# Four gate projections of each mixer as column pairs of seven half products, in a two-layer hybrid decoder trunk

## The chip, the core and the metric

The kernel runs on one core of a Trainium2 chip. The metric is the device time of one execution in microseconds (us), lower is better; of several runs the median counts. Engines are named as the profile names them: PE is TensorE (matrix products), PEld its weight loads, DVE VectorE, ACT ScalarE, POOL GpSimd, SP SyncE (which issues the weight transfers here).

## What is computed

A decoder trunk of two layers on 512 tokens, with 16 learned meta tokens ahead of them, 528 in all, and 1024 channels. A layer is a mixer and a gated MLP, each with an RMS norm before and behind it. The mixer projects its input once; the columns of that projection belong to four retention heads (with rotary positions on query and key) and four heads of gated linear attention (GLA). Every head's output is normalised and multiplied by a swish gate, `silu(rg)` or `silu(gr)`, which are columns of the same projection.

```python
proj = h @ w_in                       # 1024 -> 3600 columns
rq, rk, rv, rg, gq, gk, gv, gr, ga = jnp.split(proj, offs, axis=-1)
rq, rk = _rope(rq, pos), _rope(rk, pos)
o_ret = _head_group_norm(_retention(rq, rk, rv), ret_norm_w) * jax.nn.silu(rg)
log_a = jax.nn.log_sigmoid(ga @ gla_gate_w2 + gla_gate_b) / GLA_TAU
o_gla = _head_rms_norm(_gla(gq, gk, gv, log_a), gla_norm_w) * jax.nn.silu(gr)
m = jnp.concatenate([o_ret, o_gla], axis=-1) @ w_out
h = h + _rmsnorm(m, post_mix_norm)
u = causal_conv3(_rmsnorm(h, pre_ffn_norm) @ ffn_up)
a, g = jnp.split(u, 2, axis=-1)
h = h + _rmsnorm((gelu(a) * g) @ ffn_down, post_ffn_norm)
```

## The kernel before

**Precision and tiles.** Channels lie on the partitions, tokens in the free dimension. Each float32 operand of a large product is held as a high and a low float16 part, and a product of two such operands is three matmuls for each block of 128 input channels (`product_step`, L523 to L525). A tile of the mixer's projection is 128 columns of `w_in`, one head's `rk`, `rq`, `rv`, `rg` and so on. It is made in two halves of tokens, 0 to 232 and 232 to 528; a half is 8 blocks x 3 = 24 matmuls into a PSUM bank `pj`, three of which go round. In layer 1 the first 14 tokens of `rq`, `gq`, `rg` and `gr` are not needed, so that their first half has 218 columns.

**Weights.** SP fetches a tile's weights (`st`, 512 KB), ACT makes the high part of a `unit` of them (L122) and DVE the low part (L130). Ten units go round, and they are asked for ten ahead.

**Order of the work.** The list `TILES` gives the order of the tiles: first `ga`, `gk`, `gq`, `gv`, then `rk`, `rq`, `rv` of heads 0 and 1, `gr` 0 and 1, `rk`, `rq`, `rv` of heads 2 and 3, the four `rg`, and `gr` 2 and 3. Everything else in the mixer (retention, GLA, outputs) is written as generators that are advanced one step after each half tile (`self.advance()`, in `mixer`), so what stands between two half tiles on PE follows from how many steps each generator pauses. Each engine runs its own instructions strictly in that order; a scheduler of the framework sets it from the order of the program and its own estimates.

**A head of retention.** `rope` (L891 to L899) turns each half of `rk` and `rq`: a DVE multiply of the PSUM tile with the cosines (L895), two ACT copies that swap the halves of the channels (L896, L897, into `tmp`), a DVE multiply with the sines (L898) and a GpSimd add (L899). When the second half of `rq` is done, `ret` is started: it pauses 2 steps and then makes the scores `rs` and `rst` on PE (L908) from `rk` and `rq`, and four transposes of the keys (`ptk`, L822). GLA in the meantime makes scores level by level: its own scores (`own` on PE, the `dg` multiply on DVE, L1028), level inputs (`lvx`, L1049, L1053) and masked copies of the level scores (`lps` into `dg`, L1012, L1016).

**Half products, in the FFN.** `paired` (L1254 to L1295) makes two 128-column tiles at once with seven products of half the size in place of eight: the input channels are split in two halves, and so are the tokens (2 x 264). It needs four combinations of the quarters of the input (`input_sums`: adds L1243, differences L1248, ACT's high parts L1250, DVE's low parts L1251), weights that are sums of quarters (`PairPiece`: sums L204, high and low parts L219 and L220), and sums of the results (ACT copies L1273, DVE sums L1277). A product is 4 blocks x 3 matmuls of 264 columns (`pp`, L1265). Before the change it is used for seven pairs of tiles of layer 0's up projection and for two of layer 1's (`PAIRED`).

Of the kernel before, what the change touches and what calls it, by code (L numbers as in the profile page):

```python
# [8 lines left out]
F16 = mybir.dt.float16  # L9
# [5 lines left out]
P = 128  # L15
# [4 lines left out]
KD = D // P  # L20
# [40 lines left out]
TILES += [(nm, j) for nm in ("rk", "rq", "rv") for j in range(2)] + [("gr", 0), ("gr", 1)]  # L61
TILES += [(nm, j) for nm in ("rk", "rq", "rv") for j in range(2, 4)] + [("rg", h) for h in range(4)] + [("gr", 2), ("gr", 3)]
# [5 lines left out]
PAIRED = {0: range(9, KF, 2), 1: (8, 10)}  # L68
HK2 = KD // 2
# [153 lines left out]
class Kern:  # L223
# [495 lines left out]
    def plan(self):  # L719
        a = self.a  # L720
        self.blocks, self.key = [], {}

        def add(key, *args):
            self.key[key] = len(self.blocks)
            self.blocks.append(Block(self, key[0], *args))

        cols = {"rk": C_RK, "rq": C_RQ, "rv": C_RV, "rg": C_RG, "gk": C_GK, "gq": C_GQ, "gv": C_GV, "gr": C_GR}
        for l in range(DEPTH):
            for nm, h in TILES:
                add((l, nm, h), a["w_in"][l], KD, *((C_GA, 16) if nm == "ga" else (cols[nm] + P * h, P)))  # L730
            for i in range(KD):
                add((l, "out", i), a["w_out"][l], KD, P * i, P)
            for i in range(KF):
                if i in PAIRED[l]:
                    first = None
                    for q in range(4):
                        self.key[l, "pair", i, q] = len(self.blocks)
                        self.blocks.append(PairPiece(self, l, a["ffn_up"][l], (P * i, DFF + P * i), q, first))
                        first = first or self.blocks[-1]
                    continue  # L740
                add((l, "upa", i), a["ffn_up"][l], KD, P * i, P)
                add((l, "upg", i), a["ffn_up"][l], KD, DFF + P * i, P)
            if l < DEPTH - 1:
                for i in range(KD):
                    for kk, nk in KPARTS:
                        add((l, "dn", i, kk), a["ffn_down"][l][kk * P : (kk + nk) * P], nk, P * i, P)
                        if i == KD - 1:
                            self.blocks[-1].place = self.stage, *self.stage_of(l)
            else:
                acc = {}  # L750
                for group in PRODUCTS:
                    for kk in range(0, HK, 2):
                        for what in group:
                            self.key[l, "dn", what, kk] = len(self.blocks)
                            self.blocks.append(Quarter(self, a["ffn_down"][l], what, kk, min(2, HK - kk), acc))

# [134 lines left out]
    def rope(self, ps, dst, n0, n1):  # L891
# [3 lines left out]
        nc.vector.tensor_tensor(out=dst[:, n0:n1], in0=ps, in1=self.cosT[:, n0:n1], op=ALU.mult)  # L895
        nc.scalar.activation(b[0:64, :n], ps[64:128], AF.Copy)  # L896
        nc.scalar.activation(b[64:128, :n], ps[0:64], AF.Copy)  # L897
        nc.vector.tensor_tensor(out=b[:, :n], in0=b[:, :n], in1=self.sinT[:, n0:n1], op=ALU.mult)  # L898
# [187 lines left out]
    def mixer(self, l):  # L1086
# [52 lines left out]
        def ret(hd):  # L1139
            res = {}  # L1140
            yield from self.pause(2)
# [7 lines left out]
        def vtr(key):  # L1149
            yield from self.pause(3)  # L1150
            vnat[key] = self.v_natural(out[key], key[1] if key[0] == "rv" else None)
            yield

# [16 lines left out]
        for i, ((nm, h), half) in enumerate(seq):  # L1170
            if i == lead:
# [82 lines left out]
    def paired(self, units, at, scale, out):  # L1254
# [7 lines left out]
        def product(ps, step, i, x, more=False):  # L1262
# [6 lines left out]
            self.tick()  # L1269
# [8 lines left out]

        pa, pb = bank(), bank()
        product(pa, 0, 0, half(0, 0))  # L1280
        r1 = copied(pa)
        product(pb, 1, 0, self.xsum[1])
        r5 = copied(pb)
        product(pa, 2, 0, self.xsum[2], True)
        u2 = copied(pa)
        self.tc.add_manual_dep(self.blocks[at + UNITS].hi.ins, self.part.ins.name, mybir.DependencyInfo(mybir.DependencyClass.NoSync, mybir.DependencyReason.DATA), reason="sums first")
        product(pb, 0, 1, self.xsum[4], True)
        sum_to(1, 0, pb, u2, 1.0, ALU.subtract)
        product(pa, 1, 1, self.xsum[3], True)
# [317 lines left out]
```

## Time and profile before

| | |
|---|---|
| runs of the kernel before | 1213.61, 1214.10, 1215.82 us; median 1214.1 |
| profiled execution | 1215.84 us |
| its span in the trace | 1214.0 us |
| instructions | 26357 |
| granted clock of PE, mean | 0.995 |
| busy: PE, DVE, ACT, POOL | 1198.6, 875.5, 677.0, 173.0 us |

All times of instructions come from the profiled execution, counted from the start of its span. A row of the timeline gives the start, how long the instruction (or a run of like ones) was at work, and in brackets how long its engine idled before it and on whom it waited. Matmuls overlap, so what a matmul costs PE is the distance to the start of the next one, not its own duration. A row of a group gives the number of instructions, their busy time, the mean of one in ns, and the idle time before them.

### The profile page before, as it was taken

Reading aid. Unit: us, or ns where it says so; the run is one execution under the profiler, and the core shown is the slowest. Engines: PE = TensorE matmul, PEld = TensorE weight load, DVE = VectorE, ACT = ScalarE, POOL = GpSimd, SP = SyncE. Lnnn points to the kernel's source line nnn. Section 1 sums busy time; section 2 is a strip of 40 time slices with the busy share of each in tenths; the row PEclk is TensorE's granted clock in tenths of the full one; section 3 lists DMA queues with packets and bytes.
Section 4 is the critical chain, followed back from the end, with each engine's and each line's share of the span. In section 5 each row is a group of like instructions: output and inputs, shape, how many; then the busy total and the mean of one; then the engine's idle time right before and its main releaser. Section 6 shows DMA issues by size and latency. Waiting matters only on the chain.

```text
span 1214.0 us, 26357 instructions
## 1 busy us (share of the span) xinstructions
PE 1198.6 (99%) x10983; PEld 1011.0 (83%) x10983; DVE 875.5 (72%) x1546; ACT 677.0 (56%) x1339; POOL 173.0 (14%) x213
## 2 busy tenths in 40 slices
PE   8999999999999999999999999999999999999997
PEld 7888889979888888989898788899888888886444
DVE  5687855378998998633566858552799998897677
ACT  6675444564876666432447644445657676564442
POOL 2122411143000000000331314112430000000001
PEclk9999999999999999999999989999999999999999
DMA  8942231113613434333333331311323363305462
GB/s 223 265 115 83 60 88 53 36 54 87 174 36 93 118 94 121 109 98 87 88 89 94 98 87 55 88 53 36 88 70 105 106 173 103 108 1 179 171 222 79
DMA packets 207004, 124.04 MB, mean 102 GB/s; under 512 B 6865, under 2 KB 194437, under 8 KB 206885
## 3 DMA queue, kind: packets, MB, share of 16 engines
q1 hardware_dynamic: 206292, 121.37, 34.5%
q8 instruction: 86, 1.41, 0.5%
q0 software_dynamic: 160, 0.52, 0.1%
q10 hardware_dynamic: 432, 0.46, 0.1%
q14 instruction: 34, 0.27, 0.1%
HBM read 120.24 MB, written 2.10 MB: 101 GB/s over the span
## 4 chain that ended last, share of the span: by engine, by line
PE 82%; DVE 9%; ACT 4%; issue 3%; DMA 1%; POOL 1%; SPq 0%; POOLq 0%; DVEq 0%; ACTq 0%
PE pu L525 10%; PE pu L523 10%; PE pu L524 10%; PE pp L1265 7%; PE pj L523 6%; PE pj L524 6%; PE pj L525 6%; PE pd L523 3%; PE pd L525 3%; PE pd L524 3%; PE po L523 2%; PE po L524 2%; PE po L525 2%; PE pl L1449 2%; DVE unit L130 1%
## 5 line engine op out<-in xcount | busy, mean ns | idle before, releaser
L525 PE MATMUL pu<-every,unit 128*128 128x296 f16 (+2 forms) x1120 | 306.9, 274 | 0.0
L524 PE MATMUL pu<-every,unit 128*128 128x296 f16 (+2 forms) x1120 | 306.9, 274 | 0.0
L523 PE MATMUL pu<-every,unit 128*128 128x296 f16 (+2 forms) x1120 | 306.3, 274 | 0.0
L523 PEld LDWEIGHTS <-unit 128*128 128x128 f16 x2572 | 253.7, 99 | 36.8
L525 PEld LDWEIGHTS <-unit 128*128 128x128 f16 x2572 | 252.1, 98 | 37.3
L524 PEld LDWEIGHTS <-unit 128*128 128x128 f16 x2572 | 252.2, 98 | 36.5
L524 PE MATMUL pj<-every,unit 128*128 128x296 f16 (+2 forms) x888 | 245.1, 276 | 0.0
L523 PE MATMUL pj<-every,unit 128*128 128x296 f16 (+2 forms) x888 | 244.9, 276 | 0.0
L525 PE MATMUL pj<-every,unit 128*128 128x296 f16 (+2 forms) x888 | 244.7, 276 | 0.0
L130 DVE SCALAR_TENSOR_TENSOR unit<-st,unit 128x1024 f16<-128x1024 f32 (+1 forms) x165 | 199.7, 1217 | 45.5 <-ACT unit L122 45.3
L122 ACT ACTIVATE unit<-st 128x1024 f16<-128x1024 f32 x163 | 169.4, 1042 | 52.0 <-PE pj L525 15.6
L447 POOL TENSOR_TENSOR every<-every 128x5 f32<-128x5 f32 (+6 forms) x31 | 38.8, 1252 | 558.3 <-DVE every L446 471.9
L481 DVE TENSOR_TENSOR acc<-acc,sq 128x296 f32<-128x296 f32 (+2 forms) x60 | 35.8, 596 | 74.2 <-ACT sq L479 71.6
L525 PE MATMUL pd<-av,unit 128*128 128x232 f16 (+1 forms) x308 | 84.8, 276 | 0.0
L524 PE MATMUL pd<-av,unit 128*128 128x232 f16 (+1 forms) x308 | 84.7, 276 | 0.0
L523 PE MATMUL pd<-av,unit 128*128 128x296 f16 (+1 forms) x308 | 84.7, 276 | 0.0
L1265 PEld LDWEIGHTS <-unit 128*128 128x128 f16 x756 | 74.0, 98 | 11.1
L1322 ACT ACTIVATE u<-pu 128x296 f32<-128x296 f32 (+2 forms) x140 | 52.8, 377 | 53.1 <-PE pu L525 53.0
L1449 PE MATMUL pl<-unit,fk 128*128 128x512 f16 x330 | 71.4, 379 | 0.0
L1311 DVE SCALAR_TENSOR_TENSOR cg<-u,every,cg 128x527 f32<-128x527 f32 (+1 forms) x88 | 66.3, 754 | 4.7 <-ACT cg L1306 4.3
L525 PE MATMUL po<-merged,unit 128*128 128x296 f16 (+2 forms) x256 | 69.7, 274 | 0.0
L524 PE MATMUL po<-merged,unit 128*128 128x296 f16 (+2 forms) x256 | 69.7, 274 | 0.0
(277 smaller groups left out, 1903.2 us busy)
## 6 DMA issues: line engine op xcount, KB each, us to landing
st<-in_ffn_up SPq DMA_DIRECT2D x70, 512.0 KB, 3.9
st<-in_w_in SPq DMA_DIRECT2D x56, 512.0 KB, 4.9
st<-in_ffn_down SPq DMA_DIRECT2D x46, 512.0 KB, 4.6
st<-in_ffn_up SPq DMA_DIRECT2D x36, 256.0 KB, 3.5
st<-in_w_out SPq DMA_DIRECT2D x16, 512.0 KB, 4.2
st<-in_ffn_down SPq DMA_DIRECT2D x8, 384.0 KB, 3.5
out<-yo SPq DMA_DIRECT2D x7, 256.0 KB, 2.1
w<-in_ffn_down SPq DMA_DIRECT2D x3, 512.0 KB, 4.8
```

Of the source, the lines that this page charges most:

```text
L122: self.hi = self.kern.nc.scalar.activation(self.unit[:, 0], self.st, AF.Copy, scale=SW)
L130: self.last = self.kern.nc.vector.scalar_tensor_tensor(out=out, in0=x, scalar=SW, in1=high, op0=ALU.mult, op1=ALU.subtract)
L447: nc.gpsimd.tensor_tensor(out=r[:w, :n], in0=t[:w, :n], in1=self.mhalf[:w, :n], op=ALU.pow)
L481: self.summed = eng.tensor_tensor(out=acc[:, :n], in0=acc[:, :n], in1=sq[:, :n], op=ALU.add)
L523: nc.tensor.matmul(ps[:, :n], w[:, 0, kk, :], x[:, 0, n0:n1], start=first, stop=False)
L524: nc.tensor.matmul(ps[:, :n], w[:, 0, kk, :], x[:, 1, n0:n1], start=False, stop=False)
L525: nc.tensor.matmul(ps[:, :n], w[:, 1, kk, :], x[:, 0, n0:n1], start=False, stop=last)
L1265: mm = lambda p, q, **kw: nc.tensor.matmul(ps, u[:, p, k, :], x[k][:, q], skip_group_check=more, **kw)
L1311: nc.vector.scalar_tensor_tensor(out=to, in0=u[:, max(lo, d) - d : L - d], scalar=self.cvec[:, ci(i) : ci(i) + 1], in1=to, op0=ALU.mult, o ...
L1322: nc.scalar.activation(u[:, n0:n1], ps[:, : n1 - n0], AF.Copy, scale=IXW)
L1449: mm = lambda x, w, **kw: nc.tensor.matmul(ps[:, cols], x, w[:, cols], skip_group_check=more, **kw)
```

## The change

In both mixers, two pairs of neighbouring gate tiles, (`rg` 0, `rg` 1) and (`gr` 2, `gr` 3), are made by `paired`: 7 x 12 = 84 matmuls of 264 columns in place of four halves of 24 matmuls each. Their weights come as four `PairPiece`s in place of two units (`pair`, a helper that the FFN now uses too). `mixer_sums` makes the four input combinations, a quarter of the blocks at a time, as a generator that is started when the first half of `rv` of head 1 is reached in the program, and that pauses two steps in each round. The pairs' results are scaled and summed as in the FFN, then ACT applies Silu in place to each tile of 528 columns. A list of seven `beats` says how often the generators are advanced after each product. `gr` 0 and `gr` 1 move back: after the retention tiles now come the pair of `rg` 0 and 1, `gr` 0, the pair of `gr` 2 and 3, then `rg` 2, `gr` 1, `rg` 3. In `rope` the two ACT copies are issued before the cosine multiply, and `ret` pauses 3 steps in place of 2. Outside the mixers the program is the same. The lines of the file shift by 1 to 8 up to `mixer` (L895 is now L905, after the copies at L903 and L904; L898 is L906, L908 is L916, L1028 is L1036) and by some 50 behind it.

```diff
-TILES += [(nm, j) for nm in ("rk", "rq", "rv") for j in range(2)] + [("gr", 0), ("gr", 1)]
-TILES += [(nm, j) for nm in ("rk", "rq", "rv") for j in range(2, 4)] + [("rg", h) for h in range(4)] + [("gr", 2), ("gr", 3)]
+TILES += [("rk", 0), ("rk", 1), ("rq", 0), ("rq", 1), ("rv", 0), ("rv", 1), ("rk", 2), ("rk", 3), ("rq", 2), ("rq", 3), ("rv", 2), ("rv", 3), ("rg", 0), ("rg", 1), ("gr", 0), ("gr", 2), ("gr", 3), ("rg", 2), ("gr", 1), ("rg", 3)]
...
+SUMS = "rv", 0
+GATED = ("rg", 0), ("gr", 2)
...
+                if (nm, h) in GATED:
+                    self.pair((l, "pair", nm, h), a["w_in"][l], (cols[nm] + P * h, cols[nm] + P * (h + 1)))
+                if (nm, h) in GATED or (nm, h - 1) in GATED:
+                    continue
...
         b = self.sm([P, WN], "tmp")
-        nc.vector.tensor_tensor(out=dst[:, n0:n1], in0=ps, in1=self.cosT[:, n0:n1], op=ALU.mult)
         nc.scalar.activation(b[0:64, :n], ps[64:128], AF.Copy)
         nc.scalar.activation(b[64:128, :n], ps[0:64], AF.Copy)
+        nc.vector.tensor_tensor(out=dst[:, n0:n1], in0=ps, in1=self.cosT[:, n0:n1], op=ALU.mult)
         nc.vector.tensor_tensor(out=b[:, :n], in0=b[:, :n], in1=self.sinT[:, n0:n1], op=ALU.mult)
...
-            yield from self.pause(2)
+            yield from self.pause(3)
             yield from self.ret_scores(out["rk", hd], out["rq", hd], res)
...
+        def gate_pair(nm, h):
+            both = out[nm, h], out[nm, h + 1] = [self.g([P, L], F32, nm) for _ in range(2)]
+            self.paired(lambda q: self.block(l, "pair", nm, h, q), self.key[l, "pair", nm, h, 0], IXW, both, sums, [0, 1, 0, 1, 0, 1, 1])
+            for i in (1, 0):
+                nc.scalar.activation(out[nm, h + i], out[nm, h + i], AF.Silu)
+                done(nm, h + i)
...
+            if (nm, half) == SUMS:
+                self.spawn(self.mixer_sums(sums)) if h == 1 else None
+            if (nm, h) in GATED or (nm, h - 1) in GATED:
+                if (nm, h) in GATED and not half:
+                    gate_pair(nm, h)
+                continue
...
+    def mixer_sums(self, out):
...
+        for k in range(HK2):
...
+            nc.vector.tensor_tensor(out=f, in0=xh[:, k::HK2, 0], in1=xh[:, k::HK2, 1], op=ALU.add)
+            x = lambda a, b: f[:, b, LT * a : LT * (a + 1)]
+            sub(s[:, 2], x(0, 0), x(1, 0))
+            sub(s[:, 0], x(1, 0), x(1, 1))
+            yield from self.pause(1)
+            sub(s[:, 1], s[:, 0], x(0, 0))
+            nc.vector.tensor_tensor(out=s[:, 3], in0=s[:, 1], in1=x(0, 1), op=ALU.add)
+            nc.scalar.activation(t[:, 0], s, AF.Copy)
+            nc.vector.tensor_tensor(out=t[:, 1], in0=s, in1=t[:, 0], op=ALU.subtract)
...
+            yield from self.pause(1)
```

What moves on the engines is shown at two places. The first is DVE in layer 1, from the end of the norms in front of the mixer to GLA's own scores. The last `every<-tmp,every` is the norm's last instruction, `gaT` and `nl` belong to GLA's decay, `dg<-every,own` are the own scores. Before:

```order
L452 TENSOR_TENSOR every<-tmp,every 128x296 x4
L130 SCALAR_TENSOR_TENSOR unit<-st,unit 128x1024
L785 SCALAR_TENSOR_TENSOR gaT<-pj,gaT 32x296
L130 SCALAR_TENSOR_TENSOR unit<-st,unit 128x1024 x4
L965 TENSOR_SCALAR nl<-z,every 128x296 x2
L975 SCALAR_TENSOR_TENSOR nl<-nl,ne 128x528 x2
L130 SCALAR_TENSOR_TENSOR unit<-st,unit 128x1024
L1028 TENSOR_TENSOR dg<-every,own 128x512 x2
```

and after, from the same instruction on, the first twelve rows:

```order
L453 TENSOR_TENSOR every<-tmp,every 128x296 x4
L1286 TENSOR_TENSOR mf<-every 128x1056
L1281 TENSOR_TENSOR msum<-mf 128x264 x2
L1281 TENSOR_TENSOR msum<-msum,mf 128x264
L1292 TENSOR_TENSOR msum<-msum,mf 128x264
L1286 TENSOR_TENSOR mf<-every 128x1056
L131 SCALAR_TENSOR_TENSOR unit<-st,unit 128x1024
L793 SCALAR_TENSOR_TENSOR gaT<-pj,gaT 32x296
L131 SCALAR_TENSOR_TENSOR unit<-st,unit 128x1024
L1294 TENSOR_TENSOR mxs<-msum,mxs 128x1056
L131 SCALAR_TENSOR_TENSOR unit<-st,unit 128x1024
L1281 TENSOR_TENSOR msum<-mf 128x264 x2
```

The scheduler puts the input sums (`mf`, `msum`, `mxs`) as early as their input is there; three of the four rounds' adds and differences, and two of the low parts, stand before `dg<-every,own` now.

The second place is DVE around the rotation of the second half of `rq`, head 0, in layer 1. Before:

```order
L895 TENSOR_TENSOR rq<-pj,room 128x296
L1012 COPY_PREDICATED dg<-every,lps 128x256
L1016 COPY_PREDICATED room<-every,lps 16x8
L1012 COPY_PREDICATED dg<-every,lps 128x256
L1016 COPY_PREDICATED room<-every,lps 16x8
L130 SCALAR_TENSOR_TENSOR unit<-st,unit 128x1024
L1012 COPY_PREDICATED dg<-every,lps 128x256
L898 TENSOR_TENSOR tmp<-tmp,room 128x296
```

and after:

```order
L905 TENSOR_TENSOR rq<-pj,room 128x296
L906 TENSOR_TENSOR tmp<-tmp,room 128x296
L1020 COPY_PREDICATED dg<-every,lps 128x256
L1024 COPY_PREDICATED room<-every,lps 16x8
L1020 COPY_PREDICATED dg<-every,lps 128x256
L1024 COPY_PREDICATED room<-every,lps 16x8
L1020 COPY_PREDICATED dg<-every,lps 128x256
```

The sine multiply (L898, now L906) stands directly behind the cosine multiply; the level copies and the unit that stood between them stand behind it.

More of the change, by code (lines that the diff above doesn't have):

```diff
@@ L734, in plan @@
                 if i in PAIRED[l]:
[L735 to L739, printed above, removed]
+                    self.pair((l, "pair", i), a["ffn_up"][l], (P * i, DFF + P * i))
                     continue
@@ L755, in plan, with pair @@
                             self.blocks.append(Quarter(self, a["ffn_down"][l], what, kk, min(2, HK - kk), acc))
+    def pair(self, key, src, cols):
+        first = None
+        for q in range(4):
+            self.key[*key, q] = len(self.blocks)
+            self.blocks.append(PairPiece(self, key[0], src, cols, q, first))
+            first = first or self.blocks[-1]
     def block(self, *key, ahead=AHEAD):
@@ L1152, in vtr @@
             yield
+        sums = [[] for _ in range(5)]
+        def gate_pair(nm, h):
[4 more added lines that the diff above has]
+                done(nm, h + i)
         def done(nm, h):
@@ L1252, in input_sums, with paired @@
             yield
-    def paired(self, units, at, scale, out):
+    def mixer_sums(self, out):
+        nc = self.nc
+        xh = self.xroom.bitcast(F16).rearrange("p (k i n) -> p k i n", k=KD, i=2)
+        sub = lambda o, x, y: nc.vector.tensor_tensor(out=o, in0=x, in1=y, op=ALU.subtract)
+        for k in range(HK2):
+            f = cell(self.keep, [P, 2, L], F32, "mf", "mf", 1)
+            s = cell(self.keep, [P, 4, LT], F32, "msum", "msum", 1)
+            t = cell(self.keep, [P, 2, 4, LT], F16, "mxs", "mxs", HK2)
+            nc.vector.tensor_tensor(out=f, in0=xh[:, k::HK2, 0], in1=xh[:, k::HK2, 1], op=ALU.add)
[7 more added lines that the diff above has]
+            nc.vector.tensor_tensor(out=t[:, 1], in0=s, in1=t[:, 0], op=ALU.subtract)
+            for i in range(4):
+                out[i + 1].append(t[:, :, i])
+            yield from self.pause(1)
+    def paired(self, units, at, scale, out, xsum=None, beats=None):
         nc = self.nc
@@ L1268, in product @@
                 mm(1, 0, start=False, stop=k == HK2 - 1)
-            self.tick()
+            if beats is None:
+                self.tick()
+            else:
+                for _ in range(beats.pop(0)):
+                    self.advance()
         def copied(ps):
@@ L1281, in paired @@
         r1 = copied(pa)
[L1282 removed]
+        product(pb, 1, 0, xsum[1])
         r5 = copied(pb)
[L1284 removed]
+        product(pa, 2, 0, xsum[2], True)
         u2 = copied(pa)
         self.tc.add_manual_dep(self.blocks[at + UNITS].hi.ins, self.part.ins.name, mybir.DependencyInfo(mybir.DependencyClass.NoSync, mybir.DependencyReason.DATA), reason="sums first")
[L1287 removed]
+        product(pb, 0, 1, xsum[4], True)
         sum_to(1, 0, pb, u2, 1.0, ALU.subtract)
[L1289 removed]
+        product(pa, 1, 1, xsum[3], True)
         sum_to(1, 1, pa, r5, -1.0, ALU.add)
```

1 line of the change is left out of this document (added).

## The prediction

> **What bounds the kernel now.** I read the page first (busy shares, granted clock, chain), then the waits of TensorE, then the timeline where the one long wait lies.
>
> The page's head, the granted clock by slice of 30.35 us, and the chain by engine:
> ```profile
> span 1214.0 us, 26357 instructions
> PE 1198.6 (99%) x10983; PEld 1011.0 (83%) x10983; DVE 875.5 (72%) x1546; ACT 677.0 (56%) x1339; POOL 173.0 (14%) x213
> ...
> PEclk9999999999999999999999989999999999999999
> ...
> PE 82%; DVE 9%; ACT 4%; issue 3%; DMA 1%; POOL 1%; SPq 0%; POOLq 0%; DVEq 0%; ACTq 0%
> ```
> TensorE is busy for 99% of the span. So time can go in two ways only: fewer columns through TensorE, or fewer of its gaps. The clock falls below full speed in one slice, the 29th. The longest row of TensorE's waits (sum, times, longest):
> ```profile
> PE rs L908 <- POOL rq L899: 3.7, 3, 3.0
> ```
> The only long wait in a mixer is that of the retention scores (rs) for the rotated query: 3.7 us in three places, 3.0 of them in one. TensorE's timeline there, in layer 1, head 0:
> ```profile
> 689.82 0.26 PE L524 MATMUL pj<-every,unit 128*128 128x218 f16 x1
> ...
> 691.96 0.29 PE L523 MATMUL pj<-every,unit 128*128 128x296 f16 x1
> ...
> 694.86 0.29 PE L525 MATMUL pj<-every,unit 128*128 128x296 f16 x1
> 695.19 0.39 PE L908 MATMUL rst<-rq,rk 128*128 128x16 f32 x2
> 695.65 0.46 PE L908 MATMUL rs<-rq,rk 128*128 128x128 f32 x2
> 699.10 1.65 PE L908 MATMUL rs<-rq,rk 128*128 128x128 f32 x6 [2.99 <-POOL rq L899]
> ```
> And what this wait goes back to, on DVE, GpSimd and ScalarE:
> ```profile
> 694.41 0.45 DVE L895 TENSOR_TENSOR rq<-pj,room 128x296 f32<-128x296 f32 x1
> ...
> 697.66 0.50 DVE L898 TENSOR_TENSOR tmp<-tmp,room 128x296 f32<-128x296 f32 x1
> ```
> ```profile
> 698.24 0.81 POOL L899 TENSOR_TENSOR rq<-rq,tmp 128x296 f32<-128x296 f32 x1 [3.10 <-DVE tmp L898]
> ```
> ```profile
> 699.12 0.35 ACT L896 ACTIVATE tmp<-pj 64x218 f32<-64x218 f32 x1 [3.39 <-DVE rq L895]
> ```
> The rotation is a chain: DVE's cosine multiply (L895), ScalarE's two copies, DVE's sine multiply (L898), GpSimd's add (L899). ScalarE's copy starts only behind the cosine multiply, and it idles 3.39 us for that. The sine multiply then stands behind other DVE work: 3.25 us from L895 to L898. And DVE ran late as it was: the half that L895 takes at 694.41 had left TensorE before 689.82. What the place costs, against the same place of layer 0, is in the stretches (length, then busy time of PE, PEld, DVE, ACT, POOL, then clock, DMA):
> ```profile
> 695.19:705.41 10.22, 7.16 (x38) 6.11 (x39) 6.94 (x17) 3.69 (x8) 2.19 (x3) 0.67 0.33 95
> 94.80:99.15 4.35, 4.19 (x40) 3.96 (x39) 4.04 (x10) 2.81 (x6) 2.14 (x3) 1.00 0.45 124
> 646.70:665.47 18.77, 18.77 (x153) 14.85 (x151) 10.06 (x12) 14.22 (x21) 3.96 (x2) 1.00 0.44 113
> 665.47:697.66 32.19, 30.53 (x319) 26.18 (x316) 27.04 (x56) 21.69 (x41) 10.05 (x12) 1.00 0.36 100
> 697.66:712.00 14.34, 12.90 (x144) 11.17 (x144) 8.44 (x20) 5.43 (x10) 3.10 (x5) 0.76 0.26 74
> ```
> The first two rows hold the same work (scores, four transposes, 24 matmuls of 232 columns): 10.22 against 4.35, so 5.9 us are lost. Part is the 2.99 us of idling. The rest is the clock: (1 - 0.76) x 14.34 = 3.4 us' worth in the last row's stretch. A wait of 3 us thus costs about as much again behind it.
>
> **Fewer columns.** Rows that give the time from one matmul to the next (with the three above):
> ```profile
> 96.77 0.26 PE L523 MATMUL pj<-every,unit 128*128 128x232 f16 x1
> ...
> 99.15 0.29 PE L523 MATMUL pj<-every,unit 128*128 128x296 f16 x1
> ```
> ```profile
> 367.67 1.51 PE L1265 MATMUL pp<-every,unit 128*128 128x264 f16 x12
> 369.02 1.51 PE L1265 MATMUL pp<-xs,unit 128*128 128x264 f16 x12
> ```
> 232 columns: 24 in 2.38 us, 99 ns each. 296: 23 in 2.90, 126 ns. 218: 23 in 2.14, 93 ns. 264, as the FFN's half products run already: 12 in 1.35, 112.5 ns. A pair of gates costs today 2 x 24 x (99 + 126) = 10.8 us in layer 0 and 2 x 24 x (93 + 126) = 10.5 in layer 1. As seven half products it is 84 x 112.5 = 9.45. Two pairs a layer save 2 x (1.35 + 1.05) = 4.8 us. TensorE's other matmuls are the same in number; only their order changes.
>
> **What is added for it.** These groups of the FFN do the same kinds of work (count | busy, mean ns):
> ```profile
> L1243 DVE TENSOR_TENSOR xf<-every 128x1056 f32<-128x1056 f16 x4 | 4.9, 1249 | 0.0
> L1331 DVE TENSOR_TENSOR fk<-fk 128x256 f32<-128x256 f32 x11 | 4.6, 415 | 0.1
> L204 DVE TENSOR_TENSOR st<-st 128x512 f32<-128x512 f32 x36 | 24.7, 686 | 0.3
> L220 DVE SCALAR_TENSOR_TENSOR unit<-st,unit 128x512 f16<-128x512 f32 x45 | 30.2, 685 | 3.9 <-ACT unit L219 3.9
> L130 DVE SCALAR_TENSOR_TENSOR unit<-st,unit 128x1024 f16<-128x1024 f32 x154 | 190.6, 1243 | 42.0 <-ACT unit L122 41.8
> ```
> Input sums, once a mixer: 4 x (1.25 + 4 x 0.42 + 1.25) = 16.7 us of DVE. Weight pieces, per pair: one large piece 1.24, four sums 4 x 0.69, five half pieces 5 x 0.685 = 7.4, less two plain units of 1.24: +4.9. Output sums: three instructions a pair on 128x264, like the 128x256 row 0.42 each: 1.3. Together 16.7 + 2 x 6.2 = 29 us more of DVE in each mixer. Only what stands in front of a rotation can reach TensorE. The pieces belong to pairs at the mixer's end and queue behind the first rotations but for the first few, in DVE's idle time (28% of the span). In layer 0 all is hidden, as its rotation waited little and head 0's scores now come 24 matmuls (2.38 us) later. If that cover were gone, each us of DVE lateness at rs would be a us of the span. The gate pair's results also come from DVE before ScalarE's Silu, some 1 us later than a plain tile's; the plain gate tile behind each pair (5.4 us) covers that, and the two other gates moved back do not wait for anything new. The last gate of the mixer is now rg 3; I allow 0 to 1 us a layer for the merge behind it.
>
> **The rotation and the scores in layer 1.** Three things pull apart. (a) The scores of head 0 are asked for 2.38 us later: the second group at 695.65 + 2.4 = 698.0 instead of 695.65. To be in time, L898 must start by about 698.0 - 0.6 (L898 to the add's start) - 0.86 = 696.6. (b) ScalarE's copies no longer wait for DVE, so the sine multiply stands directly behind the cosine multiply: the up to 3.25 us between them shrink to 0.4. Where DVE isn't late, the cosine multiply now waits for two copies (0.35 us each by the row above); that costs nothing as long as DVE runs behind TensorE. (c) The sums: three adds, twelve differences and two low parts (11.3 us), with one more unit (1.24), now stand on DVE between the norms' end (646.70) and the own scores' multiply (665.47). That stretch had 18.77 - 10.06 = 8.7 us idle, so the multiply comes up to 3.8 us later; I take 2 to 4. Between it and L898 stand another add, four differences and two low parts (5.4 us), but the 3.25 us between L895 and L898 and some level work now stand behind L898. I count this as even with today's 27.04 us busy of 32.19, with 2 us of sums more as the other end. How much of the 5.15 us idle there can be filled, no row shows: none gives L898 at 697.66 + 2 to 4 = 700 to 702; all gives 694.5 to 696.5. I take half, 698.1, since part of that idling was the wait for copies that (b) ends. That is 1.5 us too late for rs: bounds 0 and 7.
>
> A wait of 1.5 us lies between this one, which brought the slow clock, and one further on that didn't:
> ```profile
> 760.26 0.94 PE L908 MATMUL rs<-rq,rk 128*128 128x128 f32 x6 [0.55 <-POOL rq L899]
> ```
> It is nearer to 0.55, so I price the clock at 0, with 3.4 as the other end. The place then costs 1.5 instead of 5.9: -4.4. The two smaller waits (0.55, and 0.16 in layer 0) go: -0.7.
>
> One effect speaks against (c). Rows of DVE, with GpSimd's add between:
> ```profile
> 693.49 1.00 DVE L898 TENSOR_TENSOR tmp<-tmp,room 128x218 f32<-128x218 f32 x1
> ...
> 699.86 0.39 DVE L898 TENSOR_TENSOR tmp<-tmp,room 128x218 f32<-128x218 f32 x1 [0.77 <-ACT tmp L897]
> ```
> ```profile
> 693.30 0.94 POOL L899 TENSOR_TENSOR rk<-rk,tmp 128x296 f32<-128x296 f32 x1 [0.40 <-DVE tmp L898]
> ```
> The same multiply took 1.00 us while GpSimd's add ran (to 694.24) and 0.39 alone. The new sums have two SBUF operands like it. GpSimd is busy 3.96 us in the first stretch, in two instructions; held for all of them, L898 would come up to 4 us later still. [...] I leave it out of the sum, as many of the sums run beside no GpSimd work, and make it a rival.
>
> **The sum.** -4.8 - 4.4 - 0.7, and +0.5 for new small waits at the mixers' ends (0 to 2): -9.4. The profiled execution took 1215.84 us (span 1214.0), so 1206.4 on its footing. It is 1.7 above the median of the runs, 1214.1 (1213.61 to 1215.82). If the runs differ by this very wait, the changed kernel's are at 1206.4; if by something else, at 1204.7. I take 1205.5.
>
> **The rivals.**
> *The wait stays whole.* DVE, held by GpSimd's adds and filled with sums, brings L898 as late against rs as today, and only the columns are saved, with the 0.7 at most: 1215.84 - 5.5 = 1210.3, less half of 1.7: 1209.5. For it: DVE is busy 84% in the stretch and ran over 4.5 us behind TensorE. Against it: (a) and (b) give 2.4 and up to 2.8 us.
> *Nothing is left of it.* DVE fills its idle time: -4.8 - 5.9 - 0.7 = -11.4, so 1204.4, or 1202.7 from the median; I say 1203. For it: the idle time in front of L898 was largely its own copies.
> *Slower: the sums choke layer 1.* If DVE can't fill its idle time, since it waits in order for ScalarE, half of the 12.5 + 5.4 us of sums reach L898: 9 us late, 6.6 beyond (a). The idling grows to 2.99 + 6.6 = 9.6, with the clock's 3.4: 13 against 5.9, so +7.1 - 4.8 = +2.3, and some more at head 1: about 1218. It decides from about 7 us of lateness on. Against it: 8.7 us idle stand right where most sums go.
> *It does not do what it says:* the half products wait for pieces or sums, and the columns' gain goes in gaps, the rest as in the first rival: about 1214. Nothing in the FFN's pairs shows that.
>
> **How the numbers follow.** The forecast 0.52, the wait whole 0.20, nothing left 0.17, choked 0.07, no gain 0.04. A measurement can tell about 0.2% (2.4 us) from no change. Faster: the first three, but for 0.01 of the second: 0.88. Same: most of the last and what is missing of the choked case's lower end: 0.05. Slower 0.07. The range takes in the first three cases: 1202 (nothing left, from the lower footing) to 1211 (the wait whole, with the ends' 1 us).
>
> **What would show it.** Right: half products of the mixers 112.5 ns apart without gaps; the clock at 9 in every slice; ScalarE's L896 (now L904) no longer waiting for DVE; rs waiting under 2 us in layer 1. Wrong: a wait of 3 us or more anywhere in a mixer with a slow slice behind it, or half products that wait for weight pieces.

## The result and the profile after

| | median, us | lowest to highest | runs | profiled execution | its span |
|---|---|---|---|---|---|
| before | 1213.87 | 1211.90 to 1215.82 | 13 | 1215.84 | 1214.0 |
| after | 1217.08 | 1216.38 to 1217.77 | 13 | 1216.70 | 1214.9 |

The ratio is 1.0024 (95% interval 1.0016 to 1.0033): the change makes the kernel slower by 3 us. The forecast was 1205.5, in a range of 1202 to 1211. The profiled execution of the kernel before lies 2.0 us above its median, that of the changed kernel 0.4 below, so the spans differ by only 0.9 us.

The head of the page after the change, the granted clock by slice, and the chain by engine:

```profile
span 1214.9 us, 26426 instructions
PE 1195.6 (98%) x10935; PEld 1006.6 (83%) x10935; DVE 929.3 (76%) x1638; ACT 696.3 (57%) x1371; POOL 181.4 (15%) x209
...
PEclk9999999999999999999999999999999999999999
...
PE 89%; DVE 5%; ACT 2%; issue 2%; DMA 1%; POOL 0%; POOLq 0%; DVEq 0%; SPq 0%; ACTq 0%
```

By this page the change worked: 48 matmuls fewer, the slow slice gone (the 24th of the forty slices before, not the 29th as the prediction has it), the chain more on TensorE than before. DVE gained 53.8 us of work. That the span is no shorter shows only in TensorE's waits (sum, times, longest):

```profile
PE lps L1010 <- DVE dgr L917: 3.0, 1, 3.0
PE ptv L812 <- ACT gv L1118: 2.3, 1, 2.3
...
PE lps L1010 <- DVE rq L905: 0.9, 1, 0.9
```

The wait at `rs` is no longer in this list. Two new ones are, and neither is at a rotation. `lps` are the level scores of GLA, `ptv` the transposes of a head's values. The two rows left out lie outside the mixers, and rows of 0.7 us and less follow. TensorE's timeline at the first, in layer 0, and at the second, in layer 1:

```profile
97.50 1.14 PE L916 MATMUL rs<-rq,rk 128*128 128x128 f32 x8
...
103.07 0.59 PE L1010 MATMUL lps<-lvx 64*128 64x8 f16 x30 [0.86 <-DVE rq L905]
106.65 0.56 PE L1010 MATMUL lps<-lvx 64*128 64x8 f16 x17 [3.00 <-DVE dgr L917]
...
677.52 0.27 PE L812 MATMUL ptv<-every,gv 128*128 128x128 f32 x1
680.05 1.11 PE L812 MATMUL ptv<-every,gv 128*128 128x128 f32 x4 [2.26 <-ACT gv L1118]
```

The first of them asks for a PSUM bank that `rs` (started at 97.50) still holds until DVE's `dgr` has read it. The second asks for `gv`, which ScalarE copies from PSUM. ScalarE's own timeline in front of it:

```profile
665.13 1.08 ACT L1293 ACTIVATE mxs<-msum 128x1056 f16<-128x1056 f32 x1 [2.58 <-DVE msum L1292]
...
679.61 0.39 ACT L1118 ACTIVATE gv<-pj 128x296 f32<-128x296 f32 x1
```

The copy of the sums first holds ScalarE for 2.58 us until DVE has made them; from there on ScalarE has no idle time up to the copy of `gv`, 2.1 us after TensorE was through with that half and went to `ptv` (677.52); another copy of sums is among what stands in between.

At the end of each wait the granted clock fell to half for 3.41 us (length, busy time of PE, PEld, DVE, ACT, POOL, clock, DMA):

```profile
60.70:91.05 30.35, 30.35 (x319) 26.34 (x318) 30.29 (x59) 26.79 (x47) 7.13 (x7) 1.00 0.43 120
106.46:109.87 3.41, 3.22 (x42) 2.63 (x42) 3.38 (x9) 0.64 (x2) 0.86 (x1) 0.50 0.00 0
668.00:697.00 29.00, 26.74 (x222) 22.34 (x221) 28.26 (x51) 26.60 (x46) 7.99 (x8) 0.94 0.39 104
679.90:683.31 3.41, 3.26 (x14) 2.34 (x15) 3.41 (x8) 3.40 (x8) 0.00 (x0) 0.50 0.00 0
```

A digit of the page stands for 30.35 us, so that 3.41 us at half speed leave it at 9; they cost 1.7 us each all the same. The first and third rows show what stands in front of the two waits: DVE is busy for 30.29 of 30.35 us in layer 0, and for 28.26 of 29.00 in layer 1. The same two stretches before the change:

```profile
60.70:91.05 30.35, 30.35 (x320) 26.43 (x318) 24.84 (x49) 23.75 (x42) 8.75 (x9) 1.00 0.41 115
668.00:697.00 29.00, 28.00 (x297) 23.95 (x294) 25.01 (x50) 19.17 (x37) 10.05 (x12) 1.00 0.36 100
```

DVE's idle time there was 5.5 and 4.0 us, and the added work used it up.

Where the span went, taken between the first own scores (`own`) and the first `pu` (first up projection of the MLP) on TensorE: layer 0 takes 209.57 us in place of 205.56 (271.57 - 62.01 against 267.39 - 61.83), layer 1 206.57 in place of 209.45. From the first layer's `pu` to the second's `own` both take 394.92. So layer 1 gained 2.9 us, where the prediction's terms have 7.0 (2.1, 4.4 and 0.55), and layer 0, where they have 2.9 (2.7 and 0.16), lost 4.0.

### The profile page after: what moved, and what is told of

Its sections match the earlier page's. It is cut to its first block, busy times and chain, and to the rows that moved or that the text cites. A ratio compares the mean times of both kernels' runs of the same rounds, so it can differ in the third digit from the quotient of the medians.

```text
span 1214.9 us, 26426 instructions
## 1 busy us (share of the span) xinstructions
PE 1195.6 (98%) x10935; PEld 1006.6 (83%) x10935; DVE 929.3 (76%) x1638; ACT 696.3 (57%) x1371; POOL 181.4 (15%) x209
## 4 chain that ended last, share of the span: by engine, by line
PE 89%; DVE 5%; ACT 2%; issue 2%; DMA 1%; POOL 0%; POOLq 0%; DVEq 0%; SPq 0%; ACTq 0%
PE pp L1310 10%; PE pu L526 10%; PE pu L524 10%; PE pu L525 10%; PE pl L1499 8%; PE pj L524 5%; PE pj L525 5%; PE pj L526 5%; PE pd L525 3%; PE pd L524 3%; PE pd L526 3%; PE po L524 2%; PE po L526 2%; PE po L525 2%; PE o L846 1%
## 5 line engine op out<-in xcount | busy, mean ns | idle before, releaser
L131 DVE SCALAR_TENSOR_TENSOR unit<-st,unit 128x1024 f16<-128x1024 f32 (+2 forms) x157 | 190.4, 1221 | 39.3 <-ACT unit L123 39.2
L524 PE MATMUL pj<-every,unit 128*128 128x296 f16 (+2 forms) x760 | 210.1, 277 | 0.7 <-ACT rv L1118 0.7
L525 PE MATMUL pj<-every,unit 128*128 128x296 f16 (+2 forms) x760 | 210.2, 277 | 0.0
L526 PE MATMUL pj<-every,unit 128*128 128x296 f16 (+2 forms) x760 | 210.1, 277 | 0.0
L123 ACT ACTIVATE unit<-st 128x1024 f16<-128x1024 f32 x155 | 161.1, 1041 | 51.7 <-PE pd L526 17.8
```

Of the source, the lines that this page charges most:

```text
L123: self.hi = self.kern.nc.scalar.activation(self.unit[:, 0], self.st, AF.Copy, scale=SW)
L131: self.last = self.kern.nc.vector.scalar_tensor_tensor(out=out, in0=x, scalar=SW, in1=high, op0=ALU.mult, op1=ALU.subtract)
L524: nc.tensor.matmul(ps[:, :n], w[:, 0, kk, :], x[:, 0, n0:n1], start=first, stop=False)
L525: nc.tensor.matmul(ps[:, :n], w[:, 0, kk, :], x[:, 1, n0:n1], start=False, stop=False)
L526: nc.tensor.matmul(ps[:, :n], w[:, 1, kk, :], x[:, 0, n0:n1], start=False, stop=last)
```

## The experiments

The theory after this comparison: the rotation's part and the columns bring what was forecast, and the added DVE work takes it back at two places. In layer 0 the weight pieces of the first pair stand on DVE in front of the score multiply (`dgr`), and the matrix of scores holds a PSUM bank that `lps` needs. In layer 1 the input sums keep DVE full, ScalarE's copy of them (`mxs`) waits for DVE, and the copy of `gv`, for which `ptv` waits, stands behind it on ScalarE. The rivals: the half products gain nothing by themselves; the new order of the gates costs the time; the weight pieces cost it and not the sums, or the reverse; or it is a matter of where pieces and sums stand, which can be mended. Every kernel was timed in five rounds beside the kernel before, whose median was 1214.59 us with the first four, 1214.55 with the next four, and 1214.48 with the last four.

**The rotation alone**: the kernel before, with the two copies first and the longer pause.

```diff
-        nc.vector.tensor_tensor(out=dst[:, n0:n1], in0=ps, in1=self.cosT[:, n0:n1], op=ALU.mult)
         nc.scalar.activation(b[0:64, :n], ps[64:128], AF.Copy)
         nc.scalar.activation(b[64:128, :n], ps[0:64], AF.Copy)
+        nc.vector.tensor_tensor(out=dst[:, n0:n1], in0=ps, in1=self.cosT[:, n0:n1], op=ALU.mult)
...
-            yield from self.pause(2)
+            yield from self.pause(3)
```

> The kernel before with only the rotation's copies first and the scores one half tile later; no pairs, no input sums, old tile order. If this edit does what the forecast said (steps a and b), the 3 us wait for rs in layer 1 and its slow clock go: 5.9 us less in the profiled execution, 4 to 6 less in the median, 1208 to 1210 us. If the edit is worth nothing and the long wait of before went away for another reason, 1213 to 1214.

Measured: 1209.46 us (1209.19 to 1209.98), ratio 0.9957 (0.9945 to 0.9970), span 1207.1. The `rs` wait is gone, no slow stretch of the clock is left, and layer 1's stretch is 202.58 us in place of 209.45. This edit is worth 5.1 us by the medians, and 6.65 from one profiled execution to the other (1215.84 to 1209.19).

**The change without pairs**: the order of the gates as after, all as plain tiles.

```diff
-SUMS = "rv", 0
-GATED = ("rg", 0), ("gr", 2)
+SUMS = "", 0
+GATED = ()
```

> The changed kernel with the pairs taken out (GATED empty) and no input sums: new tile order, rotation's copies first, scores later, all gates as plain tiles. If pairs and sums are what costs, it runs like the rotation's edit alone, 1208 to 1210 us, and has neither the wait of lps in layer 0 nor that of ptv in layer 1. If the moved gates are to blame, both waits or others of 2 us or more stay, and it is at 1215 or above.

Measured: 1208.18 us (1207.83 to 1208.29), ratio 0.9946 (0.9933 to 0.9958), span 1206.0. The gates' new places cost nothing: 1.3 us less than the rotation alone, half of it in the mixers (205.16 + 202.30 against 205.64 + 202.58, 0.8 us). TensorE's waits, all of those from 1 us on; of all that are listed, none is in a mixer:

```profile
PE pts L596 <- DVE ndg L704: 1.4, 1, 1.4
PE warm L572 <- POOL every L387: 1.2, 1, 1.2
```

**The change without the input sums**: the mixers' half products take the normed input of the first quarter five times in place of its four combinations, so the four gates are not the reference's; weight pieces, half products and output sums are all there.

```diff
-            if (nm, half) == SUMS:
-                self.spawn(self.mixer_sums(sums)) if h == 1 else None
...
-        xsum = xsum or self.xsum
+        xsum = [half(0, 0)] * 5 if xsum else self.xsum
```

> The changed kernel without the input sums: the four products that need them read the input's first quarter, so the gates' values are not the reference's; all matmuls and weight pieces stay. Theory pieces: the wait of lps in layer 0 (4.2 us and the slow clock behind it, 5.9 in all) comes from the first pair's weight pieces, which stand on DVE in front of the scores' eviction; it stays, and only layer 1's wait of ptv (2.4 us and clock, 4.1) goes: 1212 to 1214 us. Theory sums: both waits come from DVE and ScalarE being late by the input sums; both go: 1206 to 1208.

Measured: 1207.33 us (1206.73 to 1208.62), ratio 0.9940 (0.9927 to 0.9952), span 1205.6. From one matmul's start to the next, the mixer's projection takes 93.10 us in plain tiles and 19.32 in half products in layer 0, together 112.42, against 114.85 without pairs; in layer 1 111.29 against 113.18. So the columns bring 2.43 + 1.89 = 4.3 us. But the span is only 0.4 shorter: `lps` takes 8.13 and 7.90 us in place of 6.29 and 6.39, and the longer of its two rows of the waits (1.1 and 0.5 us) is

```profile
PE lps L1010 <- DVE dgr L917: 1.1, 2, 0.7
```

With the sums, the change itself, the kernel is 9.75 us slower than this (1217.08, timed apart, beside a kernel before of 1213.87).

**Pairs at the end**: the first pair comes two tiles later, the second one, and the last plain gate `rg` 3 stays last.

```diff
-... ("rv", 3), ("rg", 0), ("rg", 1), ("gr", 0), ("gr", 2), ("gr", 3), ("rg", 2), ("gr", 1), ("rg", 3)]
+... ("rv", 3), ("gr", 0), ("gr", 1), ("rg", 0), ("rg", 1), ("rg", 2), ("gr", 2), ("gr", 3), ("rg", 3)]
```

> The changed kernel with the pairs two plain tiles later (gr 0 and gr 1 ahead of the pair of rg 0 and 1, rg 2 behind it), so that the first pair's weight pieces are made some 11 us later and stand behind the first scores' eviction. Theory pieces: layer 0's wait of lps goes (5.9 us), layer 1's of ptv stays: 1210 to 1212 us. Theory sums: nothing changes by over 1 us, 1216 to 1218.

Measured: 1217.64 us (1215.65 to 1218.52, 11 runs), ratio 1.0025 (1.0016 to 1.0034), span 1216.5. The rows of its waits that lie in the mixers, from 1 us on:

```profile
PE pto L889 <- DVE on L875: 4.9, 2, 2.4
PE ptv L812 <- ACT gv L1118: 2.2, 1, 2.2
...
PE pj L524 <- DVE gr L1326: 1.3, 2, 0.7
PE lps L1010 <- DVE dgr L917: 1.3, 1, 1.3
```

`lps` waits less, as the pieces are asked for two tiles later, and `ptv` as long as before, as the sums stand where they stood. But TensorE now comes to the transposes of two heads' outputs (`pto`) before DVE has made them, and plain tiles (`pj`) wait for the pairs' output sums. So a later place alone mends nothing.

**Pieces behind the scores**: the first pair's pieces are asked for seven units ahead in place of ten, and their low parts (L221) are put behind head 1's score multiply on DVE, and so behind head 0's too. It is an order only, without a wait.

```diff
+            if self.ahead < 99:
+                kern.tc.add_manual_dep(low.ins, kern.scored.ins.name, ...NoSync...)
...
+            if key[2] == "rg":
+                self.blocks[-1].ahead = 7
...
-        nc.vector.tensor_tensor(out=dg, in0=ps, in1=self.tri...)
+        self.scored = nc.vector.tensor_tensor(out=dg, in0=ps, in1=self.tri...)
```

> The changed kernel with the weight pieces of the pair of rg 0 and 1 held, by order alone, behind the eviction of head 1's scores on DVE; input sums where they were. Theory queue (both waits come from what stands on the queue ahead, be it sums or pieces): layer 0's wait of lps shrinks from 4.2 us to under 1 and its slow clock goes, layer 1's wait of ptv (2.4) stays: 1211 to 1213 us. Theory sums alone: nothing moves in layer 0, 1216 to 1218.

Measured: 1209.44 us (1208.97 to 1209.82), ratio 0.9959 (0.9946 to 0.9971), span 1207.7: 7.6 us under the change. DVE around the score multiply of layer 0, first after the change, then with the pieces behind:

```profile
97.82 1.31 DVE L221 SCALAR_TENSOR_TENSOR unit<-st,unit 128x1024 f16<-128x1024 f32 x1
99.16 0.69 DVE L205 TENSOR_TENSOR st<-st 128x512 f32<-128x512 f32 x1
...
100.39 0.69 DVE L205 TENSOR_TENSOR st<-st 128x512 f32<-128x512 f32 x1
...
103.42 1.89 DVE L221 SCALAR_TENSOR_TENSOR unit<-st,unit 128x512 f16<-128x512 f32 x2
105.24 0.68 DVE L205 TENSOR_TENSOR st<-st 128x512 f32<-128x512 f32 x1
...
105.92 0.68 DVE L917 TENSOR_TENSOR dgr<-rs,every 128x512 f32<-128x512 f32 x1
```

```profile
100.28 0.68 DVE L921 TENSOR_TENSOR dgr<-rs,every 128x512 f32<-128x512 f32 x1
...
106.09 0.69 DVE L921 TENSOR_TENSOR dgr<-rs,every 128x512 f32<-128x512 f32 x1 [0.81 <-PE rs L920]
106.69 1.22 DVE L221 SCALAR_TENSOR_TENSOR unit<-st,unit 128x1024 f16<-128x1024 f32 x1
```

With the pieces in front, `dgr` runs at 105.92, over 7 us after the scores were done at 98.64 (97.50 + 1.14), and TensorE goes on with `lps` at 106.65, as soon as it ends. With the pieces behind, head 0's runs at 100.28, the first piece comes behind head 1's (106.09), and no wait for either is left. Layer 0 then takes 203.92 us, less than without pairs (205.16). Layer 1 keeps its wait:

```profile
PE ptv L816 <- ACT gv L1122: 2.3, 1, 2.3
```

**Sums behind the scores**: the sums start at `rk` of head 2, each round's add behind the score multiply, in both layers.

```diff
-SUMS = "rv", 0
+SUMS = "rk", 0
...
-                self.spawn(self.mixer_sums(sums)) if h == 1 else None
+                if h == 2:
+                    adding = self.mixer_sums(sums)
+                    self.spawn(adding)
...
+            self.finish(adding)   # ahead of a pair
...
-            nc.vector.tensor_tensor(out=f, in0=xh[:, k::HK2, 0], in1=xh[:, k::HK2, 1], op=ALU.add)
+            both = nc.vector.tensor_tensor(out=f, in0=xh[:, k::HK2, 0], in1=xh[:, k::HK2, 1], op=ALU.add)
+            self.tc.add_manual_dep(both.ins, self.scored.ins.name, ...NoSync...)
```

> The changed kernel with the input sums held, by order alone, behind the eviction of head 1's scores, a round at a time up to the pair; pieces where they were. Theory queue: layer 1's wait of ptv goes (2.4 us and its clock, 4.1 in all), since ScalarE no longer stands before a sum's high part; layer 0 keeps the small waits of the run without sums (0.8 and 0.4): 1207 to 1210 us. If DVE has no room for the sums so late, the half products wait for them at about 163 and 767 us, by up to 5 us a layer: 1215 to 1220.

Measured: 1224.47 us (1223.88 to 1225.10), ratio 1.0082 (1.0068 to 1.0096), span 1223.3. The `ptv` wait is gone, and the mixer's middle pays more for it, with 4.1 us at `lps` in four places and, longest in sum, this at `o` (the products of a head's output, here held up by the normalising `on` of an earlier one):

```profile
PE o L846 <- DVE on L875: 4.5, 2, 2.2
```

**Both behind**: the last two edits together.

> Both edits together: input sums and the first pair's pieces behind the eviction of head 1's scores. Theory queue: none of the long waits is left, and if the half products find their sums and pieces ready, the run is the forecast's lower end, 1204 to 1207 us, below the kernel without pairs (1208.2). If DVE has no room, the half products wait and it is at 1210 or above.

Measured: 1229.88 us (1229.60 to 1230.41, 4 runs), ratio 1.0128 (1.0114 to 1.0142), span 1228.3. The two do not add up to a gain: all of the work now meets in the mixer's middle, with waits at `o` and `lps` of up to 3.0 us.

**ScalarE's copy on GpSimd**: the high parts of the sums (1.08 us each, L1293) leave ScalarE.

```diff
-            nc.scalar.activation(t[:, 0], s, AF.Copy)
+            nc.gpsimd.tensor_copy(t[:, 0], s)
```

> The changed kernel with the four high parts of the input sums made by GpSimd in place of ScalarE; everything else as it was. If layer 1's wait of ptv comes from ScalarE's queue, which stands 2.6 us before such a copy with the values' copy behind it, the wait goes (4.1 us with its clock), layer 0's lps stays: 1212 to 1214 us. If it comes from DVE being late, the wait stays or grows, as GpSimd's copies hold DVE's two-operand instructions: 1217 to 1222.

Measured: 1224.93 us (1223.98 to 1226.12, 4 runs), ratio 1.0087 (1.0073 to 1.0101), span 1224.0. The `ptv` wait goes, so it did come through ScalarE's queue. But the rotation's add stands on GpSimd, and the copy takes up to 4.75 us there, so TensorE now waits at the projection itself. TensorE's longest wait, and GpSimd:

```profile
PE pj L524 <- DVE rq L905: 11.4, 3, 4.3
```

```profile
75.93 4.75 POOL L1293 CAST mxs<-msum 128x1056 f16<-128x1056 f32 x1 [14.47 <-DVE msum L1292]
...
92.13 1.30 POOL L1293 CAST mxs<-msum 128x1056 f16<-128x1056 f32 x1
```

**No sums, pieces behind**: the third and the fifth kernel's edits together; the four gates are again not the reference's.

> The changed kernel without the input sums (the four products that need them read the input's first quarter, so the gates' values are not the reference's) and with the first pair's weight pieces behind head 1's scores: both suspects off TensorE's path. If they are all that ate the gain, the columns' 4.3 us appear against the kernel without pairs (1208.2), less some 1 us for more changes between tiles: 1204.5 to 1205.5. If the run without sums (1207.3) is already all that pairs can give, 1207.

Measured: 1205.90 us (1205.35 to 1206.64), ratio 0.9933 (0.9921 to 0.9945), span 1203.9. Nothing of a mixer is left in the waits but 1.4 us at `o`. The time is close to the prediction's 1205.5, in a kernel whose sums cost nothing and whose pieces stand out of the way; but that is in part luck. The two pairs bring only 2.2 us in the mixers even here (205.16 + 202.30 without pairs, 203.90 + 201.40 with them), not 4.3 or the forecast's 4.8: 1.4 go in the waits at `o`, and most of the rest in level scores, which take about 0.4 us a layer more among half products. The gates' new places, which the forecast did not count, bring 1.3.

**Half of layer 1's sums later**: pieces behind the scores, and layer 1's third and fourth round of sums behind the rotation's sine multiply.

```diff
+        self.turned = nc.vector.tensor_tensor(out=b[:, :n], in0=b[:, :n], in1=self.sinT...)
...
+            if l and k >= 2:
+                self.tc.add_manual_dep(both.ins, self.turned.ins.name, ...NoSync...)
```

> The changed kernel with the first pair's pieces behind head 1's scores and, in layer 1, two of the four rounds of input sums held behind the rotation of head 1. If layer 1's wait of ptv (2.4 us and clock, 3.5 in all against the run with pieces behind) comes from the sums that stand ahead of the values' copies on DVE and ScalarE, it goes or falls under 1 us, and with at most 1 us of new waits later the run is at 1206 to 1208. If the late rounds cost as in the run with all sums late, 1209 to 1212.

Measured: 1214.14 us (1213.65 to 1215.95, 11 runs), ratio 1.0001 (0.9992 to 1.0010), span 1212.1. Layer 1 takes 209.53 us in place of 205.61. The old wait only shrinks, and two come to it:

```profile
PE ptv L816 <- ACT gv L1122: 1.8, 1, 1.8
PE lps L1014 <- DVE room L922: 1.7, 1, 1.7
PE pj L526 <- ACT rv L1122: 1.6, 1, 1.6
```

**Pairs in layer 0 alone**: pieces behind the scores there, and layer 1 with plain gates.

```diff
-                if (nm, h) in GATED:
+                if l == 0 and (nm, h) in GATED:
...
-                self.spawn(self.mixer_sums(sums)) if h == 1 else None
+                self.spawn(self.mixer_sums(sums)) if h == 1 and l == 0 else None
```

> Pairs in layer 0 only, with the first pair's pieces behind head 1's scores; layer 1 has plain gate tiles in the new order. Layer 0 as in the run with pieces behind (203.9 us from own scores to the up projection), layer 1 as in the kernel without pairs (202.3): 1206.5 to 1207.5 us.

Measured: 1207.62 us (1207.41 to 1208.60), ratio 0.9949 (0.9936 to 0.9961), span 1205.6: the fastest that computes the reference. It isn't told apart from the change without pairs (1208.18; 1207.83 to 1208.29). Layer 0 takes 203.92 against 205.16 without pairs, layer 1 202.30 in both.

**Three rounds of layer 1's sums later** (`k >= 1` in place of `k >= 2`).

> As the split of layer 1's input sums, but with only one round early and three held behind the rotation of head 1. Layer 1's wait of ptv goes entirely; three late rounds (12 us of DVE in some 60 us) cost more waits around 735 to 750 us than two: 1207 to 1210 us, slower than the two-and-two split if that has no wait of ptv left, faster if it has.

Measured: 1215.17 us (1214.29 to 1215.82, 11 runs), ratio 1.0008 (0.9998 to 1.0017), span 1212.6. The `ptv` wait is gone; in its place stand about 1 us each at `lps` (two rows), `pj` and `rs`, and one at the output:

```profile
PE o L850 <- DVE on L879: 2.4, 1, 2.4
```

## Why the prediction was wrong, step by step

- **The rotation and the scores** (-4.4 and -0.7): right for the edit by itself. Between the profiled executions, from which the terms are taken, it brings 6.65 us alone; that is the 5.9 + 0.7 of "nothing is left of it", and the 5.1 that the medians give is that of the forecast only by chance. In the changed kernel the place is not free of the sums: in layer 1, head 0's rotated query is ready at 705.22 (GpSimd's add ends) and `rs` and `rst` begin at 705.61, after TensorE had lost 4.0 us at `ptv` (2.26 idle, 1.7 by the clock). DVE idled for 0.7 us from 668 to 706 and never for TensorE, so without that loss the query would have been some 3.6 us late (an estimate from these times). The kernel without pairs has the query ready 2.9 us early (693.53 against 696.44). So the rival "the wait stays whole" is out as to the edit, and in the changed kernel an earlier wait hides it.
- **Fewer columns** (-4.8): right in kind, -4.3 in size. Twelve half matmuls go in 1.35 us as in the MLP, but in 1.45 where they stand between level scores, so that 336 of them take 38.64 us where the forecast had 37.8. TensorE after the change, first pair of layer 0:

```profile
162.03 1.51 PE L1310 MATMUL pp<-every,unit 128*128 128x264 f16 x12
163.38 1.51 PE L1310 MATMUL pp<-mxs,unit 128*128 128x264 f16 x12
...
165.59 1.52 PE L1310 MATMUL pp<-mxs,unit 128*128 128x264 f16 x12
167.04 0.47 PE L1010 MATMUL lps<-lvx 64*128 64x64 f16 x20
```

- **What is added** (29 us of DVE a mixer): DVE's busy time rose by 53.8 us in two mixers, 27 each. The size was right.
- **"Only what stands in front of a rotation can reach TensorE"**: this is the step that failed, and with it "In layer 0 all is hidden". In this kernel DVE's queue also reached TensorE where DVE empties a PSUM bank that TensorE is to fill again, at the score multiply between `rs` and `lps` (3.00 us in layer 0), and where ScalarE waited for DVE and TensorE for something behind that on ScalarE (2.26 us at `ptv` in layer 1); each wait cost another 1.7 us by the clock. The waits' list before the change named DVE at none of these places in a mixer because DVE was early there, by an amount that the list does not give.
- **The pieces "queue behind the first rotations but for the first few"**: true of head 0's rotation, and no cover. A window of ten counts the tile at work, so the first pair's pieces are asked for from `rq` of head 1 on, the ninth tile in front of the pair; they came onto DVE among head 1's rotation, six instructions of L221 and L205 (5.3 us) in front of head 0's `dgr`.
- **"DVE's idle time (28% of the span)" as cover**: an average. In the stretch 60.70 to 91.05 it was 5.5 us, and with the sums (part of which stood in front of that stretch already) 0.06 us of it were left.
- **New small waits at the mixers' ends** (+0.5): the waits came in the middle. The change without pairs and the change itself differ by 8.7 us in the mixers (4.41 in layer 0, 4.27 in layer 1), where the columns should have given 4.3 the other way: 13 us in place of 0.5. In layer 0 `lps` alone has 5.5 of it (11.76 against 6.29). In layer 1 `ptv` has 3.1 (7.45 against 4.37) and `lps` 2.0 (8.41 against 6.39). Parts of these and most of the rest, some 3.5 us, are the two slow stretches of the clock.
- **The rival "the sums choke layer 1"** (1218) has almost the time that came, and that is luck: it had layer 1 lose and layer 0 gain, and it was layer 0 that lost 4.0 us, while layer 1 gained 2.9. Its cause was there, DVE full and late in layer 1, but the lateness reached TensorE at `ptv` before it could at `rs`.
- **The signs**: three of the four signs of being right came (no slow digit, the copies not waiting for DVE, no wait at `rs`) and the fourth for the most part (112.5 ns apart, but for the 1.45 us above). So did the sign of being wrong: 3.00 us at `lps` with a slow stretch behind it, too short to show in the slice's digit.

The theory behind the experiments is shown for layer 0: taking the first pair's pieces out from in front of `dgr` ends the wait, and the layer then gains 1.24 us from its pairs. It took both, though: without the sums the same pieces make a wait there of 0.7 us at most, and with the sums but later pieces there is none. For layer 1 it is shown that the sums are the cause (without them, pieces behind: 201.40 us; with them 205.61) and that the `ptv` wait comes through ScalarE's copies. Every other place for those sums that was tried (three of them) made layer 1 slower, 209.5 to 210.7 us (213.5 with the pieces late as well). The three also missed their own expectations on the slow side: 1224.5, 1214.1 and 1215.2 us where at most 1220, 1212 and 1210 was expected. That the sums are too much for DVE there wherever they stand is argued from this and from the idle time, 4.0 us in 29, and not shown; an order that fits may exist.

The interplay of the two costs was not foreseen either: moving the pieces brought 1.4 us without the sums (1207.33 to 1205.90) and 7.6 with them (1217.08 to 1209.44; timed apart). With slack in DVE's queue the pieces cost little; with the queue full they reached TensorE.

## What to carry to other kernels

Ask of work that is added to an idle engine which of its later instructions another engine waits for, PSUM banks that it empties included, and how early each is now; a list of waits shows only those that are already late. Count idle time in the stretch where the work will stand, not over the span. And where work is asked for by a count of units ahead, count again at which place it then lands in the queue.

## What the runs showed of the hardware

In these runs the clock's price depended on where a wait fell. In the kernel with the pairs at the end the same transposes wait twice, equally long. TensorE there, and then the stretches behind the two waits:

```profile
190.76 0.81 PE L889 MATMUL pto<-every,on 128*128 128x128 f32 x4 [2.44 <-DVE on L875]
...
797.02 0.81 PE L889 MATMUL pto<-every,on 128*128 128x128 f32 x4 [2.44 <-DVE on L875]
```

```profile
191.95:195.36 3.41, 3.41 (x20) 2.69 (x18) 1.63 (x7) 0.42 (x1) 0.00 (x0) 0.50 0.00 0
680.05:683.46 3.41, 3.41 (x17) 2.20 (x16) 3.41 (x7) 3.39 (x8) 0.00 (x0) 0.50 0.06 9
797.73:801.00 3.27, 3.27 (x36) 3.12 (x36) 2.11 (x8) 0.64 (x1) 0.00 (x0) 1.00 0.07 18
```

The first wait brought 3.41 us at half speed, the second nothing. The slow stretches that begin in the two mixers lie 680.05 - 191.95 = 488.10 us apart here and 679.90 - 106.46 = 573.44 after the change. 488.10 / 143 and 573.44 / 168 both give 3.413, and a single slow stretch lasted 3.41 us, so in these two traces the slow stretches lie on a grid of 3.413 us. On that grid (680.05 + 34 x 3.413 = 796.10) the first wait lies in one step for 2.2 of its 2.44 us, and the second is cut in two by the boundary at 796.10, 1.5 and 0.9 us. So what counted here was the idle share of one step, and not the length of the wait. Three steps of the kernel before, up to the end of its slow stretch, and the two steps ahead of the slow ones after the change:

```profile
694.51:697.92 3.41, 1.49 (x10) 0.86 (x7) 3.41 (x8) 0.82 (x2) 0.57 (x1) 1.00 0.00 0
697.92:701.33 3.41, 2.23 (x10) 2.23 (x11) 2.48 (x9) 2.15 (x4) 1.38 (x2) 0.50 0.53 154
701.33:704.74 3.41, 3.41 (x20) 2.63 (x19) 1.73 (x3) 1.02 (x3) 0.81 (x1) 0.50 0.24 63
```

```profile
103.05:106.46 3.41, 0.59 (x30) 0.49 (x30) 3.41 (x6) 0.77 (x2) 1.25 (x2) 1.00 0.00 0
676.49:679.90 3.41, 1.30 (x14) 1.06 (x11) 2.89 (x4) 3.41 (x6) 0.00 (x0) 1.00 0.45 127
```

TensorE idled for 1.92 us in the first of the three and for 2.8 and 2.1 in the two, and half speed followed each. After the change the steps at 99.63 and 710.62 hold 0.84 and 0.89 us of idling, and full speed followed. With half of layer 1's sums later, a wait of 1.83 us at `ptv` (up to 673.81) brought no slow stretch: the clock is at 1.00 from 671.50 to 684.00. In the kernel before, the step at half speed with 1.18 us of idling was followed by another one, and so 6.83 us went at half speed; the one without idling, and after the change those with 0.19 and 0.15, were followed by full speed.

DVE and GpSimd both took longer where the sums met GpSimd's adds, in layer 1, in front of the own scores. The two engines there, DVE first:

```profile
652.14 0.78 DVE L1281 TENSOR_TENSOR msum<-mf 128x264 f32<-128x264 f32 x2
...
660.13 1.89 DVE L1281 TENSOR_TENSOR msum<-mf 128x264 f32<-128x264 f32 x2
661.94 2.35 DVE L131 SCALAR_TENSOR_TENSOR unit<-st,unit 128x1024 f16<-128x1024 f32 x1
```

```profile
659.83 1.56 POOL L1133 TENSOR_TENSOR tots<-room 128x528 f32<-128x528 f32 x1 [18.28 <-issue]
661.90 1.30 POOL L1133 TENSOR_TENSOR tots<-room 128x528 f32<-128x528 f32 x1 [0.52 <-ACT room L1118]
```

The same pair of differences took 0.78 us alone and 1.89 with GpSimd at work from 659.83 on; the low part of a unit took 2.35 in place of the 1.25 of its group, and the first of GpSimd's two adds 1.56 where the second took 1.30. For DVE that is 2.2 us in front of the own scores' multiply, by the effect that the prediction left out of its sum. The multiply came 23.7 us after the norm's end (674.67 - 650.94) in place of 18.8, so 5.0 us later, where the prediction took 2 to 4. How much of layer 0's lateness is of this kind was not measured apart. A copy on GpSimd went with a longer sum as well: after the change there is one (L428, from 51.42 on, 1.60 us), and DVE's sum that began beside it (L1292, at 52.52) took 0.79 us, where the one at 43.65 took 0.43. In the kernel with the sums' copies on GpSimd one of them took 4.75 us and another 1.30; what DVE did beside them no row here shows.
